# Projecting q, k and z of the first layer by four heads: tokens on partitions, 512 weight columns moving, the results turned by VectorE and transfers

## The chip, the cores and the metric

The kernel runs on one core of one Trainium2 chip, in one launch. The metric is the device time of that launch in microseconds (us); a kernel's number is the median of its runs. Engines are named as the profile names them: PE is TensorE (PEld its weight loads), DVE is VectorE, ACT is ScalarE, POOL is GpSimd, SP is SyncE, which here issues the weight loads.

## What is computed

One step of a two-layer trunk in float32, for 384 tokens (256 prompt tokens of one new stream, and 16 new tokens of each of 8 running streams), width 2048. Cut to what matters here:

```python
# layer 0
h  = rmsnorm(x, norm0_g)
p  = h @ w_in0                       # 2048 x 8200: fox q, k, v, z; stick-breaking q, k, v, z; forget logits
fq, fk, fv, fz, logf, sq, sk, sv, sz = split(p)    # 8 heads of 128 on either side
o_fox = softmax(fq fk^T * scale + F_q - F_k) @ fv  # F: running sum of logf; causal; cached keys and values
o_sb  = stick_breaking(sq, sk) @ sv                # exp(log_sigmoid(z) + reverse running sum of log_sigmoid(-z))
mix = concat(o_fox * silu(fz), o_sb * silu(sz))
x   = x + mix @ w_out0
# layer 1
u, v, z = split(rmsnorm(x, norm1_g) @ w_in1)       # 3 x 4096
x = x + (u * (w_sp @ layernorm(v) + b_sp) * silu(z)) @ w_out1
y = rmsnorm(x, final_g)
```

The outputs are y, the new keys, values and log forget gates, and the normalised v rows of the running streams.

## The kernel before

Every dense product runs as three matmuls on halves of the operands: both operands are split into a rounded part `hi` and a remainder `lo`, and hi·hi, hi·lo and lo·hi are added up in one bank of the accumulator memory. ACT makes `hi` (L80, L86), DVE makes `lo` (L82, L87). Weights come in pieces of 256 KB by SP's queue (`wload`, L73; five buffers) and are split into `whi` and `wlo` (four buffers each). The normalised input is kept transposed, as sixteen blocks of 128 features by 384 tokens (`hhi`, `hlo`).

Layer 0 is worked through in eight pairs of heads (`pair(g)`, L348): g 0 to 3 are fox, 4 to 7 stick-breaking. For q, k and z a pair calls `dense_T` (L89): a 128 by 128 block of weights is stationary, the 384 tokens move, and two banks take the two heads; the result stands with the head's features on partitions, as the scores need it. It is evicted by DVE, with the rows' scale `rstd_bc` (the reciprocal root mean square, spread over all partitions by L147 to L153). Keys are also needed with tokens on partitions, for the output: `natural` (L368) transposes 32 by 32 blocks on DVE and writes the result out with 16 transfers. Values come from `values_first` (L327; 256 columns, the first two pairs) or `dense_nat` (L108; 512 columns moving, for two pairs at once), whose result has tokens on partitions.

`head` (L431) makes the scores (L455 to L460), turns them into probabilities (fox: L472 to L483, with the division by the row's sum in L483; stick-breaking: L485 to L496), transposes these on PE (L500), copies them out (`PT`, L502) and multiplies by the cached and new values (L508 to L521). The part for the running streams (`od`) is copied (L515 or L517) and transposed by PE (L518), so that `mx` has the head's features on partitions. At the end of a pair `mx` is multiplied by silu(z) (L425) and split into the blocks `mixhi`, `mixlo` (L426, by L86 and L87). The out-projection (L563) calls `dense_nat` four times over these blocks.

The accumulator memory is two pools of four banks: `d` for dense products, `a` for all else. The blocks `slot` are a pool of 16 buffers of 128 by 1536. Each engine works through its own list in order; the list is fixed when the kernel is built, by a scheduler that runs a model of the program. `tc.issue_after(i)` puts an instruction behind `i` in it.

In layer 1 the gated products are turned as follows (L673 to L684): DVE transposes the 32 by 32 blocks of a 128 by 1536 tile (`trn`, L674), sixteen transfers from POOL's queue, each 32 partitions by 12 by 32, put the blocks in place (`gTt`, L678), and ACT and DVE split the result (L683, L684).

Of the kernel before, what the change touches and what calls it, by code (L numbers as in the profile page):

```python
# [15 lines left out]
P = 128  # L16
# [10 lines left out]
NEG = -1.0e30  # L27

# [3 lines left out]
def f32(ap):  # L32
    return ap.bitcast(F32)
# [3 lines left out]
def tile_hybrid_step(  # L37
# [18 lines left out]
    splits = []  # L56
# [19 lines left out]
    def wunit(src, nk, ncols, raw=None):  # L76
# [3 lines left out]
        S.activation(hi, raw, AF.Copy)  # L80
        lo = wp.tile([P, WPITCH], F32R, tag="wlo", name=nm("wlo"))[:, :512].rearrange("p (k c) -> p k c", k=nk)
        splits.append(V.tensor_tensor(out=lo, in0=raw, in1=f32(hi), op=ALU.subtract).ins)  # L82
        return hi, lo
# [5 lines left out]
    def dense_T(w, c0, hhi, hlo, raws=(), after=None):  # L89
        out = [dbank(), dbank()]  # L90
        for u in range(KT // 2):
            with ExitStack() as order:
                if after:
                    for i in after[2 * u]:
                        order.enter_context(tc.issue_after(i.ins))
                hi, lo = wunit(w[u * 256:(u + 1) * 256, c0:c0 + 256], 2, 256, raws[u] if u < len(raws) else None)
            for kk in range(2):
                k = 2 * u + kk
                h, l = hhi[k // 4][:, k % 4, :], hlo[k // 4][:, k % 4, :]
                for cb in range(2):  # L100
                    o = out[cb][:, :T]
                    cs = slice(cb * P, (cb + 1) * P)
                    PE.matmul(o, lhsT=hi[:, kk, cs], rhs=h, start=(k == 0), stop=False)  # L103
                    PE.matmul(o, lhsT=hi[:, kk, cs], rhs=l, start=False, stop=False)  # L104
                    PE.matmul(o, lhsT=lo[:, kk, cs], rhs=h, start=False, stop=(k == KT - 1))  # L105
        return out

    def dense_nat(w, k0, c0, his, los, nk=None, between=None):  # L108

        nk = nk or len(his)  # L110
        out = [dbank() for _ in range(NT)]
        for kp in range(0, nk, 2):
            if between and kp in between:
                with tc.issue_after(splits[-1]):
                    between[kp]()
            ws = [wunit(w[(k0 + k) * P:(k0 + k + 1) * P, c0:c0 + 512], 1, 512) for k in (kp, kp + 1)]
            for tb in range(NT):
                t = slice(tb * P, (tb + 1) * P)
                for j in range(2):
                    k = kp + j  # L120
                    hi, lo = ws[j]
                    o = out[tb]
                    PE.matmul(o, lhsT=his[k][:, t], rhs=hi[:, 0, :], start=(k == 0), stop=False)  # L123
                    PE.matmul(o, lhsT=his[k][:, t], rhs=lo[:, 0, :], start=False, stop=False)  # L124
                    PE.matmul(o, lhsT=los[k][:, t], rhs=hi[:, 0, :], start=False, stop=(k == nk - 1))  # L125
        return out
# [8 lines left out]
    rstd_bc = cpool.tile([P, T], F32, name="rstd_bc")  # L135
# [3 lines left out]
    cpool.tile([P, 104], F32, name="apad")  # L139
# [7 lines left out]
    def calc_rstd_bc(pool):  # L147
        diag = pool.tile([P, T], F32, tag="z", name=nm("rdiag"))
        for tb in range(NT):
            V.tensor_scalar(out=diag[:, tb * P:(tb + 1) * P], in0=ident, scalar1=rstd[:, tb:tb + 1], scalar2=None, op0=ALU.mult)  # L150
        b = bank()
        PE.matmul(b[:, :T], lhsT=ones, rhs=diag, start=True, stop=True)
        S.activation(rstd_bc, b[:, :T], AF.Copy)  # L153

# [4 lines left out]
    def load_x(dst, c0, n):  # L159
        nc.sync.dma_start(dst[:, :2, :], xp_view[:, :, c0:c0 + n])  # L160
        nc.sync.dma_start(dst[:, 2, :], xview[2][:, c0:c0 + n])

    def transpose_scaled(src, gcol, hi, lo):

        b = bank()
        for tb in range(NT):
            PE.transpose(b[:, tb * P:(tb + 1) * P], src[tb], ident)
        return (S.activation(hi, b[:, :T], AF.Copy, scale=gcol),
                V.scalar_tensor_tensor(out=lo, in0=b[:, :T], scalar=gcol, in1=f32(hi), op0=ALU.mult, op1=ALU.subtract))


    with ExitStack() as l0:
# [4 lines left out]
        nc.sync.dma_start(graw[:, 0, :], norm0_g.rearrange("(k p) -> k p", p=P))  # L177
# [6 lines left out]
        xs, raws = [], []  # L184
        for c in range(4):
            x_t = slot(F32).rearrange("p (t c) -> p t c", t=NT)
            for j in range(2):
                load_x(x_t[:, :, j * 256:(j + 1) * 256], c * 512 + j * 256, 256)
                if len(raws) < 5:
                    u = len(raws)  # L190
                    raws.append(wload(w_in0[u * 256:(u + 1) * 256, 1024:1280], 2, 256))
            xs.append(x_t)
        hhi, hlo, done = [], [], []
        with tc.issue_after(gains(0).ins):
            for c in range(4):
                hi, lo = slot(), slot()
                hi, lo = hi.rearrange("p (k t) -> p k t", k=4), lo.rearrange("p (k t) -> p k t", k=4)
                for kk in range(4):
                    k = 4 * c + kk
                    done.append(transpose_scaled([xs[c][:, tb, kk * P:(kk + 1) * P] for tb in range(NT)], gT[:, k:k + 1], hi[:, kk, :], lo[:, kk, :]))  # L200
                hhi.append(hi)
                hlo.append(lo)
            first = dense_T(w_in0, 1024, hhi, hlo, raws, done)
        with tc.issue_after(done[-1][0].ins), tc.issue_after(done[-1][1].ins):
            for c in range(4):
                for tb in range(NT):
# [3 lines left out]
                    else:  # L210
                        sq = lp.tile([P, NT * 256], F32, tag="knat", bufs=1, name=nm("sq"))[:, :512]
# [15 lines left out]
        sums = lp.tile([P, NT * P], F32, tag="sg", bufs=1, name="sums")  # L227
# [44 lines left out]
        V.tensor_copy(wf[:, 0, 0:1], hlo[1][:, 3, 0:1].bitcast(F32))  # L272
# [49 lines left out]
        vprev = [None]  # L322
# [25 lines left out]
        def pair(g):  # L348
            fox = g < 4
            hp = g % 4  # L350
            base = (0 if fox else 4096) + hp * 256
            kc, vc = (c_fox_k, c_fox_v) if fox else (c_sb_k, c_sb_v)
            ko_p, vo_p, ko_s, vo_s = (fk_p, fv_p, fk_s, fv_s) if fox else (sk_p, sv_p, sk_s, sv_s)
            h0 = 2 * hp

            kcache = lp.tile([P, 2, 8 * P], F32, tag="kcache", bufs=1, name=nm("kcache"))
            vcache = lp.tile([P, 8, 256], F32, tag="vcache", bufs=1, name=nm("vcache"))
            def project(what, c0):
                o = first if c0 == 1024 else dense_T(w_in0, c0, hhi, hlo)
                t = lp.tile([P, 2, T], F32, tag=what, bufs=2 if what == "kT" else 1, name=nm(what))  # L360
                for cb in range(2):
                    if what == "qT":
                        V.scalar_tensor_tensor(out=t[:, cb, :], in0=o[cb][:, :T], scalar=ATTN_SCALE, in1=rstd_bc, op0=ALU.mult, op1=ALU.mult)
                    else:
                        V.tensor_tensor(out=t[:, cb, :], in0=o[cb][:, :T], in1=rstd_bc, op=ALU.mult)
                return t

            def natural(src, o_p, o_s):  # L368

                nat = lp.tile([P, 2, T // 32, 32], F32, tag="knat", bufs=1, name=nm("knat"))  # L370
                V.transpose(out=nat.rearrange("p h a d -> p (h a d)"), in_=src.rearrange("p h t -> p (h t)"))  # L371
                o_p = o_p[0].rearrange("(a p) h d -> p h a d", p=32)
                o_s = o_s.rearrange("b q h d -> (b q) h d").rearrange("(a p) h d -> p h a d", p=32)
                for j in range(4):
                    js = slice(32 * j, 32 * j + 32)
                    for hh in range(2):
                        G.dma_start(o_p[:, h0 + hh, :, js], nat[js, hh, :8, :])  # L377
                        G.dma_start(o_s[:, h0 + hh, :, js], nat[js, hh, 8:, :])  # L378

            kT = project("kT", base + 1024)  # L380
            natural(kT, ko_p, ko_s)
            if g < 2:
                nv, vnat = 256, lp.tile([P, NT, 256], F32, tag="vnat", name=nm("vnat"))
                o = values_first(base + 2048, g == 0)
            elif g % 2 == 0:
                nv, vnat = 512, lp.tile([P, NT, 512], F32, tag="vnat", name=nm("vnat"))
                o = dense_nat(w_in0, 0, base + 2048, [hk(hhi, k) for k in range(KT)], [hk(hlo, k) for k in range(KT)])
            else:
                nv, vnat = 0, vprev[0]
# [137 lines left out]
        for g in range(8):  # L527
            pair(g)
# [263 lines left out]
```

## Time and profile before

| | |
|---|---|
| runs of the kernel | 1830.46 us median of 3 (1829.74 to 1831.8) |
| the profiled execution's own time | 1831.22 us |
| its span, first to last instruction | 1829.5 us |
| granted clock of PE | 0.999 |
| busy: PE, DVE, ACT, POOL | 1811.7, 932.8, 715.3, 345.2 us |
| dense matmuls with 384 columns moving | 2304 (L103, L104, L105, 768 each) |
| dense matmuls with 512 columns moving | 5472 (L123, L124, L125, 1824 each) |
| moved by DMA | 276.25 MB, 151 GB/s over the span |

The profile shows one execution. A row of its groups reads: line, engine, operation, output<-input, shapes, number; then busy time in us and the mean in ns of one; then the idle time of that engine just before, with what ended it. In a timeline a row begins with its start and its length in us. Matmuls overlap, so the length of one is not its cost: the distance from one start to the next is.

### The profile page before, as it was taken

The numbers are of one execution on the slowest core, as the hardware profiler recorded it, in microseconds if no ns is written. First come the engines' busy times: TensorE is split into PE (matmuls) and PEld (weight loads), VectorE is DVE, ScalarE is ACT, GpSimd is POOL, SyncE is SP. The second block draws the span as 40 slices with busy tenths as digits, with TensorE's granted clock in tenths as the row PEclk, the third lists the DMA queues.
The fourth block names the chain that finished last, engine by engine and source line by source line (L and its number), as shares of the span: only waits on it lengthen the run. The fifth ranks groups of instructions, "written<-read, shape, count | busy, mean of one in ns | idle before, by whom it ended". The sixth has DMA issues, their size and how long they took to land. (4 is left out here: it accounts for less than half of the span.)

```text
span 1829.5 us, 25641 instructions
## 1 busy us (share of the span) xinstructions
PE 1811.7 (99%) x9217; PEld 1565.4 (86%) x9217; DVE 932.8 (51%) x1570; ACT 715.3 (39%) x1275; POOL 345.2 (19%) x559
## 2 busy tenths in 40 slices
PE   8999999999999999999999999999999999999997
PEld 7999899899899888888888888888888888888886
DVE  6466365456646644543443544554543563455366
ACT  5354343444535534443333333333323333333334
POOL 2553233213212002200300111320120210220020
PEclk9999999999999999999999999999999999999999
DMA  6776566565555467744544445554444554455453
GB/s 185 190 181 151 171 148 166 144 165 144 157 149 156 142 175 204 199 127 129 139 130 127 133 137 151 146 144 139 148 139 132 150 155 127 144 144 150 144 146 130
DMA packets 181871, 276.25 MB, mean 151 GB/s; under 512 B 22520, under 2 KB 87984, under 8 KB 181744
## 3 DMA queue, kind: packets, MB, share of 16 engines
q1 hardware_dynamic: 152752, 226.42, 43.1%
q0 software_dynamic: 21792, 43.87, 9.5%
q10 hardware_dynamic: 7200, 4.33, 0.7%
q8 instruction: 72, 1.18, 0.3%
q14 instruction: 55, 0.45, 0.1%
HBM read 253.50 MB, written 14.74 MB: 147 GB/s over the span
## 5 line engine op out<-in xcount | busy, mean ns | idle before, releaser
L82 DVE TENSOR_TENSOR wlo<-raw,whi 128x512 fp32r<-128x512 f32 x800 | 551.2, 695 | 767.6 <-ACT whi L80 766.4
L80 ACT ACTIVATE whi<-raw 128x512 fp32r<-128x512 f32 x800 | 504.2, 631 | 921.5 <-PE d L125 727.9
L124 PE MATMUL d<-wlo,slot 128*128 128x512 f32 x1824 | 711.7, 391 | 0.2
L125 PE MATMUL d<-whi,slot 128*128 128x512 f32 x1824 | 706.2, 389 | 0.0
L123 PE MATMUL d<-whi,slot 128*128 128x512 f32 x1824 | 632.3, 390 | 0.9 <-ACT slot L557 0.5
L123 PEld LDWEIGHTS d<-whi,slot 128*128 128x128 f32 x1824 | 342.4, 188 | 73.2 <-ACT slot L557 1.0
L124 PEld LDWEIGHTS d<-wlo,slot 128*128 128x128 f32 x1824 | 342.5, 188 | 71.7 <-DVE wlo L82 1.0
L125 PEld LDWEIGHTS d<-whi,slot 128*128 128x128 f32 x1824 | 342.5, 188 | 70.9
L105 PE MATMUL d<-slot,wlo 128*128 128x384 f32 x768 | 259.4, 338 | 0.0
L104 PE MATMUL d<-slot,whi 128*128 128x384 f32 x768 | 258.7, 337 | 0.0
L103 PE MATMUL d<-slot,whi 128*128 128x384 f32 x768 | 258.3, 337 | 0.0
L678 POOL DMA_DIRECT2D gTt<-trn x128 | 78.1, 618 | 446.4 <-issue 263.8
L105 PEld LDWEIGHTS d<-slot,wlo 128*128 128x128 f32 x768 | 144.2, 188 | 6.1 <-issue 6.0
L104 PEld LDWEIGHTS d<-slot,whi 128*128 128x128 f32 x768 | 144.6, 188 | 0.5 <-issue 0.4
L103 PEld LDWEIGHTS d<-slot,whi 128*128 128x128 f32 x768 | 144.5, 188 | 0.4
L377 POOL DMA_DIRECT2D out_dram<-knat x64 | 38.1, 596 | 113.1 <-DVE knat L371 112.9
L639 POOL DMA_DIRECT2D wr<-in_w_sp_dram x64 | 35.0, 554 | 26.7 <-DVE wT L643 25.6
L633 DVE TENSOR_TENSOR slot<-d,slot 128x512 f32<-128x512 f32 x48 | 32.2, 687 | 12.6 <-PE d L125 12.6
L404 POOL DMA_DIRECT2D kcache<-in_cache_sb_k_dram x32 | 25.0, 790 | 71.4 <-DVE KT L451 57.5
L378 POOL DMA_DIRECT2D out_dram<-knat x64 | 36.1, 563 | 0.0
L545 POOL DMA_DIRECT2D blk<-h1d x12 | 11.0, 922 | 129.0 <-DMA h1d<-slot 99.6
L596 POOL DMA_DIRECT2D slot<-in_sgu_ln_g_dram x8 | 4.5, 568 | 135.4 <-PE d L125 135.4
(220 smaller groups left out, 1189.6 us busy)
## 6 DMA issues: line engine op xcount, KB each, us to landing
raw<-in_w_in_dram SPq DMA_DIRECT2D x640, 256.0 KB, 2.8
raw<-in_w_out_dram SPq DMA_DIRECT2D x192, 256.0 KB, 3.3
gTt<-trn POOLq DMA_DIRECT2D x128, 48.0 KB, 3.4
kcache<-in_cache_fox_k_dram POOLq DMA_DIRECT2D x32, 128.0 KB, 5.3
vcache<-in_cache_fox_v_dram POOLq DMA_DIRECT2D x4, 1024.0 KB, 8.0
kcache<-in_cache_sb_k_dram POOLq DMA_DIRECT2D x32, 128.0 KB, 4.7
vcache<-in_cache_sb_v_dram POOLq DMA_DIRECT2D x4, 1024.0 KB, 6.6
h1d<-slot ACTq DMA_DIRECT2D x12, 256.0 KB, 2.8
```

Source lines behind the costliest of these rows:

```text
L80: S.activation(hi, raw, AF.Copy)
L82: splits.append(V.tensor_tensor(out=lo, in0=raw, in1=f32(hi), op=ALU.subtract).ins)
L103: PE.matmul(o, lhsT=hi[:, kk, cs], rhs=h, start=(k == 0), stop=False)
L104: PE.matmul(o, lhsT=hi[:, kk, cs], rhs=l, start=False, stop=False)
L105: PE.matmul(o, lhsT=lo[:, kk, cs], rhs=h, start=False, stop=(k == KT - 1))
L123: PE.matmul(o, lhsT=his[k][:, t], rhs=hi[:, 0, :], start=(k == 0), stop=False)
L124: PE.matmul(o, lhsT=his[k][:, t], rhs=lo[:, 0, :], start=False, stop=False)
L125: PE.matmul(o, lhsT=los[k][:, t], rhs=hi[:, 0, :], start=False, stop=(k == nk - 1))
L377: G.dma_start(o_p[:, h0 + hh, :, js], nat[js, hh, :8, :])
L378: G.dma_start(o_s[:, h0 + hh, :, js], nat[js, hh, 8:, :])
L639: G.dma_start(wr[js, 0, :].rearrange("p (a s) -> p a s", s=32), w_sp[g, :, js].rearrange("(a p) s -> p a s", p=32))
L678: G.dma_start(gT[32 * j:32 * j + 32, :, 32 * a:32 * a + 32], trn[32 * a:32 * a + 32, :, 32 * j:32 * j + 32])
```

## The change

It has five parts.

1. `dense_T` goes, and q, k and z are projected by `dense_nat`, four heads at a time (`quad(g)`, g 0 to 3): a block of 128 tokens is stationary, 512 weight columns move, and three banks hold the three blocks of tokens. ACT evicts them with the row scale (`evict`, L400 of the new kernel) into a `slot`. `turn` then does what layer 1 does: one DVE transpose of 128 by 1536 (L124) and sixteen POOL transfers (L127), for keys, queries and, at the end of a quad, for the mixed output (`mT`), which is then split by ACT (L473) and DVE (L474). `rstd_bc` goes. Keys go out with two transfers (L403, L404).
2. In `head` the output is made with tokens on partitions (three matmuls, L559 to L561; DVE writes it into `mixn`, L564 or L567, where the fox rows are divided by their sums). L483, L518 and the two ACT copies L523 and L524 go.
3. The opening is put in order by hand (`then`): transposes of x, splits and products by pairs of k, the first products beginning after two of the sixteen blocks; `graw` and two pieces of x are loaded from ACT's queue.
4. The first two of the four out-projections are taken in two steps (`early`: the twelve blocks of quads 0 to 2, with the second in banks of pool `a`; `rest`: the last four).
5. At the end three of the last weight pieces are loaded early by POOL, and the last splits lie between or behind the products of `out1(24, 4)`.

The core of the diff:

```diff
-    def dense_T(w, c0, hhi, hlo, raws=(), after=None):
...
-                    PE.matmul(o, lhsT=hi[:, kk, cs], rhs=h, start=(k == 0), stop=False)
-                    PE.matmul(o, lhsT=hi[:, kk, cs], rhs=l, start=False, stop=False)
-                    PE.matmul(o, lhsT=lo[:, kk, cs], rhs=h, start=False, stop=(k == KT - 1))
+    def products(out, his, los, ws, kp, tbs, first, last):
...
+                PE.matmul(o, lhsT=his[k][:, t], rhs=hi[:, 0, :], start=(k == first), stop=False)
+                PE.matmul(o, lhsT=his[k][:, t], rhs=lo[:, 0, :], start=False, stop=False)
+                mm = PE.matmul(o, lhsT=los[k][:, t], rhs=hi[:, 0, :], start=False, stop=(k == last))
...
+    def turn(src, dst, trn=None):
+        trn = slot(F32).rearrange("p (x d) -> p x d", d=P) if trn is None else trn
+        V.transpose(out=trn.rearrange("p x d -> p (x d)"), in_=src.rearrange("p t d -> p (t d)"))
+        for j in range(4):
+            for a in range(4):
+                G.dma_start(dst[32 * j:32 * j + 32, :, 32 * a:32 * a + 32], trn[32 * a:32 * a + 32, :, 32 * j:32 * j + 32])
...
-        calc_rstd_bc(lp)
+        V.tensor_scalar(out=rstdq, in0=rstd, scalar1=ATTN_SCALE, scalar2=None, op0=ALU.mult)
...
+            def project(c0):
+                return first if c0 == 1024 else dense_nat(w_in0, 0, c0, h0h, h0l)
+            def evict(o, dst, scale, n=512):
+                for tb in range(NT):
+                    S.activation(dst[:, tb, :], o[tb][:, :n], AF.Copy, scale=scale[:, tb:tb + 1])
...
+            def turned(c0, scale, tag, outs=None):
+                nat = slot(F32).rearrange("p (t c) -> p t c", t=NT)
+                evict(project(c0), nat, scale)
+                if outs:
+                    store(nat, *outs)
+                t = lp.tile([P, NT * 4, P], F32, tag=tag, bufs=1, name=nm(tag))
+                turn(nat, t)
+                return t.rearrange("p (t h) q -> p h t q", h=4), nat
...
+            for hh in range(4):
+                hs = slice(hh * P, hh * P + P)
+                head(g, h0 + hh, kT[:, hh], vnat[:, :, hs], qT[:, hh], *cached(hh), mixn[:, :, hs])
+            zn = big("gz")
+            evict(project(base + 3072), zn, rstd)
...
+                V.tensor_tensor(out=z, in0=z, in1=mixn[:, tb, :], op=ALU.mult)
+            t = lp.tile([P, NT * 4, P], F32, tag="qT", bufs=1, name=nm("mT"))
+            turn(zn, t)
...
+            for k in range(4):
+                h3 = mixhi[g][:, k, :].rearrange("p (t q) -> p t q", q=P)
+                S.activation(h3, mT[:, k], AF.Copy)
...
-            PE.transpose(od[:, P:2 * P], os_, ident)
...
-        for g in range(8):
-            pair(g)
+        for g in range(4):
+            quad(g)
...
+        early, rest = range(0, 12, 2), range(12, KT, 2)
+        outs = [[dbank() for _ in range(NT)], [bank() for _ in range(NT)]]
```

How it moves instructions, at three places. First PE at the end of a group of heads. Before, behind the second head of pair 0 (L520 and L521 are the products of its prompt part), the dense products of pair 1's values go on in banks that are already theirs:

```order
L508 MATMUL a_1055<-vnat_494,PT_1053 32x128 x4
L512 MATMUL a_1055<-vcache_472,PT_1053 32x128 x8
L520 MATMUL a_1071<-PT_1040,vnat_494 128x256
L521 MATMUL a_1071<-PT_1040,vnat_494 128x128
L344 MATMUL d_1411<-wlo_1585,slot_206 128x256
L345 MATMUL d_1411<-whi_1584,slot_207 128x256
```

Now, at the end of quad 0, its fourth head (scores L503 to L508, transposes L545, products L553 to L561) and what follows it; `d_2211` to `d_2213` are the banks of the query projection of quad 1, and `d_1943` to `d_1945` (not in these rows) those of its key projection, complete by then:

```order
L508 MATMUL a_1589<-KT_1584,qT_1308 32x256 x2
L101 MATMUL d_2211<-whi_2246,slot_120 128x512
L102 MATMUL d_2211<-wlo_2248,slot_120 128x512
L103 MATMUL d_2211<-whi_2246,slot_121 128x512
L101 MATMUL d_2211<-whi_2252,slot_120 128x512
L102 MATMUL d_2211<-wlo_2254,slot_120 128x512
L103 MATMUL d_2211<-whi_2252,slot_121 128x512
L545 MATMUL a_1605<-ident,pr_1601 128x128 x3
L545 MATMUL a_1618<-ident,pr_1615 128x128 x3
```

```order
L559 MATMUL a_1637<-vnat_590,PT_1609 128x128
L560 MATMUL a_1637<-vnat_590,PT_1609 128x128
L561 MATMUL a_1637<-vnat_590,PT_1609 128x128
L101 MATMUL d_2212<-whi_2216,slot_120 128x512
L102 MATMUL d_2212<-wlo_2218,slot_120 128x512
```

Six dense matmuls stand between the fourth head's scores and its transposes, and behind its last product comes the first one into `d_2212`, a bank that the key projection held: pool `d` has four.

Second, ACT at the same place: the copies of the fourth head, the split of the turned output, the three evictions of the key projection, a weight split.

```order
L547 ACTIVATE PT_1609<-a_1605 128x384
L547 ACTIVATE PT_1622<-a_1618 128x384
L473 ACTIVATE slot_1932<-mT_1913 128x384 x4
L400 ACTIVATE slot_1942<-d_1943,rstd 128x512
L400 ACTIVATE slot_1942<-d_1944,rstd 128x512
L400 ACTIVATE slot_1942<-d_1945,rstd 128x512
L84 ACTIVATE whi_2276<-raw_2274 128x512
```

The evictions stand behind the split of `mT`, which needs all sixteen transfers. Before, at the end of pair 0, the evictions (here of pair 1's values) stood ahead of the split of the last head's output (`slot_1233<-mx_1074`):

```order
L523 ACTIVATE mx_1074<-a_1071 128x256
L392 ACTIVATE vnat_1410<-d_1411,rstd 128x256
L392 ACTIVATE vnat_1410<-d_1412,rstd 128x256
L392 ACTIVATE vnat_1410<-d_1413,rstd 128x256
L80 ACTIVATE whi_1678<-raw_1676 128x512
L524 ACTIVATE mx_1074<-a_1055 128x128
L86 ACTIVATE slot_1233<-mx_1074 128x384
```

Third, PE's opening, before (L167 are transposes of x, `d_232` and `d_233` the first two banks):

```order
L167 MATMUL a_142<-ident,slot_95 128x128
L167 MATMUL a_148<-ident,slot_95 128x128
L167 MATMUL a_156<-ident,slot_104 128x128 x3
L167 MATMUL a_162<-ident,slot_104 128x128 x3
L167 MATMUL a_168<-ident,slot_104 128x128 x3
L103 MATMUL d_232<-slot_128,whi_234 128x384
```

and now (L211 are the transposes):

```order
L211 MATMUL a_131<-ident,slot_95 128x128 x3
L211 MATMUL a_137<-ident,slot_95 128x128 x3
L101 MATMUL d_128<-whi_143,slot_120 128x512
L102 MATMUL d_128<-wlo_145,slot_120 128x512
L103 MATMUL d_128<-whi_143,slot_121 128x512
L101 MATMUL d_128<-whi_147,slot_120 128x512
```

The first dense product stands behind two blocks' transposes, where it stood behind seven.

More of the change, by code (lines that the diff above doesn't have):

```diff
@@ L27 @@
 NEG = -1.0e30
+APAD = 96
 WPITCH = 576
@@ new lines, in dense_nat @@
+    def dense_nat(w, k0, c0, his, los, nk=None, between=None, out=None, ks=None):
+        nk = nk or len(his)
+        out = out or [dbank() for _ in range(NT)]
+        for kp in range(0, nk, 2) if ks is None else ks:
+            behind = ()
+            if between and kp in between:
+                with tc.issue_after(splits[-1]), tc.issue_after(highs[-1]):
+                    behind = between[kp]() or ()
+            ws = [wunit(w[(k0 + k) * P:(k0 + k + 1) * P, c0:c0 + 512], 1, 512, behind=behind) for k in (kp, kp + 1)]
+            products(out, his, los, ws, kp, range(NT), 0, nk - 1)
+        return out
@@ L145, in calc_rstd, with load_x @@
         G.tensor_tensor(out=rstd, in0=tot, in1=ex, op=ALU.pow)
[L147 to L153, printed above, removed]
     xview = [x_prompt[0, 0:P, :], x_prompt[0, P:2 * P, :], x_sample.rearrange("b q c -> (b q) c")]
     xp_view = x_prompt.rearrange("o (t p) c -> p (o t) c", p=P)
-    def load_x(dst, c0, n):
+    def load_x(dst, c0, n, q=None):
         nc.sync.dma_start(dst[:, :2, :], xp_view[:, :, c0:c0 + n])
[L161 to L169, printed above, removed]
+        (q or nc.sync).dma_start(dst[:, 2, :], xview[2][:, c0:c0 + n])
     with ExitStack() as l0:
@@ L194, in tile_hybrid_step @@
[L194 to L203, printed above, removed]
+        tail = {}
@@ new lines, in tile_hybrid_step, with x_transposes @@
+        load_piece(0)
+        load_raw()
+        load_raw()
+        load_piece(1)
+        load_raw()
+        load_raw()
+        load_piece(2)
+        load_raw()
+        load_piece(3)
+        tail["DVE"] = gains(0).ins
+        hhi, hlo = [], []
+        for c in range(4):
+            hhi.append(slot().rearrange("p (k t) -> p k t", k=4))
+            hlo.append(slot().rearrange("p (k t) -> p k t", k=4))
+        def x_transposes(k):
+            b = bank()
+            for tb in range(NT):
+                then("PE", lambda: PE.transpose(b[:, tb * P:(tb + 1) * P], xs[k // 4][:, tb, k % 4 * P:k % 4 * P + P], ident))
+            gcol = gT[:, k:k + 1]
+            hi, lo = hhi[k // 4][:, k % 4, :], hlo[k // 4][:, k % 4, :]
+            return (then("ACT", lambda: S.activation(hi, b[:, :T], AF.Copy, scale=gcol)),
+                    then("DVE", lambda: V.scalar_tensor_tensor(out=lo, in0=b[:, :T], scalar=gcol, in1=f32(hi), op0=ALU.mult, op1=ALU.subtract)))
@@ new lines, in first_unit @@
+        def first_unit(k):
+            hi = wp.tile([P, WPITCH], F32R, tag="whi", name=nm("whi"))[:, :512].rearrange("p (k c) -> p k c", k=1)
+            then("ACT", lambda: S.activation(hi, raws[k], AF.Copy))
+            lo = wp.tile([P, WPITCH], F32R, tag="wlo", name=nm("wlo"))[:, :512].rearrange("p (k c) -> p k c", k=1)
+            splits.append(then("DVE", lambda: V.tensor_tensor(out=lo, in0=raws[k], in1=f32(hi), op=ALU.subtract)).ins)
+            return hi, lo
+        h0h = [hhi[k // 4][:, k % 4, :] for k in range(KT)]
```

329 lines of the change are left out of this document (163 added, 166 removed).

## The prediction

> **What bounds the kernel now.** I read the page's first two parts, then the waits of PE, then timelines of PE at places where the change acts.
>
> ```profile
> span 1829.5 us, 25641 instructions
> PE 1811.7 (99%) x9217; PEld 1565.4 (86%) x9217; DVE 932.8 (51%) x1570; ACT 715.3 (39%) x1275; POOL 345.2 (19%) x559
> PE   8999999999999999999999999999999999999997
> PE a L167 <- DMA slot<-in_x_prompt_dram: 4.8, 3, 2.6
> PE a L181 <- DMA graw<-in_norm_g_dram: 2.5, 1, 2.5
> PE d L721 <- DVE slot L633: 1.3, 1, 1.3
> PE d L123 <- ACT slot L557: 0.5, 1, 0.5
> PE d L123 <- DVE slot L567: 0.3, 1, 0.3
> ```
>
> PE is full from the opening to the tail. Its waits add up to 9.4 us (4.8 + 2.5 + 1.3 + 0.5 + 0.3), and the last three are all there is behind the opening. So the change can win only by fewer or cheaper matmuls, an earlier start or a shorter tail, and it loses whatever new idle time it gives PE. The page's span stands 1.7 us below the execution's own 1831.22 us, and that 0.8 us above the median of the runs; I sum against 1831.2 and take 0.8 off at the end. A difference of 0.2% (3.7 us) is about what a measurement of this kernel can tell from none.
>
> **Dense matmuls.** The price is the pitch from start to start.
>
> ```profile
> 71.10 0.33 PE L105 MATMUL d<-slot,wlo 128*128 128x384 f32 x1
> ...
> 72.83 0.33 PE L103 MATMUL d<-slot,whi 128*128 128x384 f32 x1
> 899.89 0.39 PE L124 MATMUL d<-wlo,slot 128*128 128x512 f32 x1
> ...
> 903.29 0.39 PE L123 MATMUL d<-whi,slot 128*128 128x512 f32 x1
> L105 PE MATMUL d<-slot,wlo 128*128 128x384 f32 x768 | 259.4, 338 | 0.0
> L518 PE MATMUL a<-ident,os 128*128 128x128 f32 x16 | 4.3, 271 | 0.0
> ```
>
> Between the first two rows lie ten steps, 0.173 us each; between the next two fifteen, 0.2267 us each. Removed: 3 x 768 = 2304 steps of 0.1733, 399.3 us. Added: 12 projections of 16 x 9 = 144 products, 1728 of 0.2267, 391.7 us. That is **−7.5**: per column moved the two differ little (0.451 and 0.443 ns). The sixteen L518 go; alone they show 4.3 us, overlapped perhaps 0.11 each: **−1.8** (0 to −4.3). L520 with its two products and L559 to L561 move the same 384 columns: nothing. L483 and L523/L524 leave engines that are half idle: nothing.
>
> **The opening.**
>
> ```profile
> 0.79 1.28 ACT L47 ACT_TABLE_LOAD   x1 [0.79 <-PEq L779]
> 0.80 0.39 SPq L177 DMA_DIRECT2D graw<-in_norm_g_dram  x1
> 4.41 1.54 PE L167 MATMUL a<-ident,slot 128*128 128x128 f32 x6 [1.67 <-DMA slot<-in_x_prompt_dram]
> ...
> 12.73 0.67 PE L103 MATMUL d<-slot,whi 128*128 128x384 f32 x1
> 13.20 0.52 PE L104 MATMUL d<-slot,whi 128*128 128x384 f32 x1
> 13.52 0.52 PE L103 MATMUL d<-slot,whi 128*128 128x384 f32 x1
> 13.84 0.44 PE L104 MATMUL d<-slot,whi 128*128 128x384 f32 x1
> L153 ACT ACTIVATE rstd_bc<-a 128x384 f32<-128x384 f32 x1 | 0.5, 493 | 4.8 <-PE a L152 4.8
> ```
>
> The first six transposes start at 4.41, dense work at 12.73. Now products may follow those six and one round of splits. `graw`, issued at 0.80 by SP, is now issued by ACT behind its table load, which ends at 2.07, and the first piece of the running streams' x behind it: up to 1.3 later. Together about 8.5, **−4** (0, if loads hold it, to −5). In exchange the first eviction needs `rstd`, which comes after the squares, and only one bank is free meanwhile; before, ACT had 4.8 us of waiting for the same scale. **+2.5** (0 to 4.8). The tail's 1.3 and the two small gaps may go: **−2** (0 to −2.1).
>
> **The end of a quad.** This decides. By the new order ACT reaches the evictions of the next quad's keys (L400) only behind the split of `mT` (L473), and PE's next product needs a bank that such an eviction frees. So PE waits through the whole turn of the fourth head's output, and behind ACT's wait stand also the weight splits. The turn is in the trace, in layer 1:
>
> ```profile
> 1087.21 1.77 DVE L674 STREAM_TRANSPOSE trn<-gate 128x1536 f32<-128x1536 f32 x1
> 1089.28 9.75 POOL L678 DMA_DIRECT2D gTt<-trn x16 [53.37 <-DVE trn L674]
> L678 POOL DMA_DIRECT2D gTt<-trn x128 | 78.1, 618 | 446.4 <-issue 263.8 <-DVE wlo L82 129.2 <-DVE trn L674 53.4
> DMA to landing us min/median/max: 1.9/3.4/5.0
> 1783.75 1.75 ACT L683 ACTIVATE slot<-gTt 128x384 fp32r<-128x384 f32 x4
> L586 ACT ACTIVATE vt<-d,rstd 128x512 f32<-128x512 f32 x24 | 16.3, 690 | 12.0 <-PE d L125 12.0
> L633 DVE TENSOR_TENSOR slot<-d,slot 128x512 f32<-128x512 f32 x48 | 32.2, 687 | 12.6 <-PE d L125 12.6
> L515 DVE TENSOR_SCALAR os<-a,st 128x128 f32<-128x128 f32 x8 | 2.8, 349 | 4.1 <-PE a L512 4.1
> ```
>
> From the fourth head's last product: three writes of 0.349 and three products with silu(z) of 0.687 on DVE, of which about 0.4 lies beside PE's last matmuls, 2.7; the transpose 1.77; sixteen transfers 9.75; the last one's landing 3.4 less its own issue, 2.8; the split of four blocks 1.75; one eviction 0.69. That is 19.5, with five handovers between engines **20 us** (17.5 with the shortest landing and no handovers, 22 with the longest). Layer 1 pays nothing for it, since PE has other products there.
>
> What PE still has to do meanwhile, from the new order: at the end of quad 0 nothing, its twelve products into the one free bank being used up; of quad 1, 57 products, 12.9 us; of quad 2 nothing again. Hence 20, 7.1 and 20.
>
> The fourth head itself loses its cover too, since its scores and transposes stand almost side by side:
>
> ```profile
> 115.06 0.60 PE L455 MATMUL a<-kT,qT 128*128 128x256 f32 x2
> ...
> 116.03 0.64 PE L460 MATMUL a<-KT,qT 128*32 128x256 f32 x8
> ...
> 120.07 0.60 ACT L476 ACTIVATE pr<-z,st 128x384 f32<-128x384 f32 x1
> ...
> 124.72 0.87 ACT L502 ACTIVATE PT<-a 128x384 f32<-128x384 f32 x2 [1.12 <-PE a L500]
> 413.70 0.60 PE L455 MATMUL a<-kT,qT 128*128 128x256 f32 x2
> ...
> 420.88 0.53 ACT L496 ACTIVATE pr<-z 128x384 f32<-128x384 f32 x1 [1.05 <-DVE z L494]
> ...
> 426.09 0.51 ACT L496 ACTIVATE pr<-z 128x384 f32<-128x384 f32 x1
> ```
>
> A fox head takes 5.6 us from its first score to its last exponential (115.06 to 120.67); less 1.6 of scores (to 116.67) and six products of 0.2267 that is 2.6, and 0.5 for the copy of the probabilities: 3 at quad 0. A stick-breaking head took 7.7 to the first exponential and 12.9 to the second. The bare case, quad 3's last head, has no dense product between scores and transposes: I take 10.5, between the two, less 1.6 for scores, plus 0.5: 9.5 (7 to 12). In quad 2 some 35 products lie beside it, 8 us: 2.4. Quad 3's own turn lies beside the early products of the second out-projection, 12 blocks by 9, 108 of 0.2267 or 24.5 us behind the last head: I take that as covered, at up to 4 if not.
>
> Together 3 + 20 + 7.1 + 2.4 + 20 + 9.5 = **+62**.
>
> Behind such a wait PE is slow at first. In the opening's rows the 384-column products from 13.20 to 13.84 stand 0.32 apart instead of 0.173, though the granted clock reads 1.00 there; the three steps from 12.73 cost 1.11 instead of 0.52. I take 1 us for each of four long waits, **+4** (2.4 to 7). The Trainium skill's page "TensorE: Matmul & The Clock Gate", section "Why this matters for your kernels", says to leave no PE-idle gaps over about 3 us between bursts, else PE goes back to half its rate; it speaks against this change. The opening's pitch agrees. If, by that page's Part 1, half the rate lasts for 3.4 us each time, 1.7 us are lost each time, and the sum would be 2.8 us higher.
>
> **Sum.** −7.5 − 1.8 − 4 + 2.5 − 2 + 62 + 4 = +53.2: 1831.2 + 53.2 = 1884.4, less 0.8: **1883.6 us**. The low ends (three turns 2.5 shorter, the bare heads 2.5 shorter, clock 2.4, no `rstd` wait, L518 at 4.3) give about 1867; the high ends (turns 2 longer, heads 2.5 longer, clock 7, no gain in opening and tail, `rstd` 4.8, quad 3's turn 4) about 1907.
>
> **Rivals.**
>
> Hidden turns, faster: were the four turns and last heads beside other products, as layer 1's are, only −7.5 − 1.8 − 4 + 2.5 − 2 = −12.8 would be left, 1817.6. It needs 20 us of products, some 88 of them, between a fourth head's last product and the first one into a bank still held. For it: L678's transfers in layer 1 cost PE no wait. Against: the order has 0, 57 and 0. 0.05.
>
> Cheap issue: if the sixteen transfers were issued beside each other, so that the turn took 1.77 and one landing of 3.4, each of the three waits would be some 9 shorter (the second gone): 62 − 9 − 7.1 − 9 = 37, about 1858.5. The row of L678 speaks against it, 618 ns each on POOL one after the other, 9.75 for sixteen. The Trainium skill's page "DMA: Bandwidth & Descriptors", section "Issuing engines are not separate DMA queues", says that the time to initiate is usually small relative to the DMA itself; for these small transfers the trace disagrees, 9.75 us of issue against 3.4 of landing. 0.06.
>
> POOL held up, slower still: ahead of `mT`'s transfers POOL's list holds the next quad's cache loads.
>
> ```profile
> L404 POOL DMA_DIRECT2D kcache<-in_cache_fox_k_dram x32 | 25.1, 794 | 13.0 <-DVE KT L451 12.3 <-DVE vcache L401 0.7
> L406 POOL DMA_DIRECT2D vcache<-in_cache_fox_v_dram x4 | 3.7, 923 | 15.6 <-PE a L512 15.6
> ```
>
> Four of 0.794 and one of 0.923 make a head's set, 4.1 us. Its value load waits for the fourth head's last cached product; if the set is issued only then, up to 4.1 at each of three quads come in front, less the 4.5 of DVE work beside it: nothing if one set, but with two sets 3.7 each, 11 in all, 1894.7. With the ends of the other terms, over 1908. 0.06.
>
> No difference: gains and waits cancel if the waits are 13 us in all, which no row suggests: 0.02.
>
> **How the numbers follow.** Forecast 0.81, cheap issue 0.06, POOL 0.06, hidden 0.05, cancelled 0.02. The forecast's bounds, 1867 to 1907, with half of each neighbouring case make the range 1856 to 1908. Faster by over 0.2%: 0.05. Within: 0.02. Slower: 0.93.
>
> **What would show it.** In the profile after, PE's waits name ACT's L400 for about 20, 7 and 20 us at the ends of quads 0, 1 and 2, with ACT idle until the transfers of `mT` and POOL busy with L127 for 9.75 us before; DVE or ACT of the last stick-breaking head holds L545 for about 9 us. Dense products start near 8.5 us. PE's busy share falls to about 96%. The forecast is wrong if those waits are under 10 us, if new waits of that size stand elsewhere, or if products of 512 columns in layer 0 don't come at 0.227 us.

## The result, and the profile after

The changed kernel takes 1888.93 us (median of 4 runs, 1888.49 to 1889.66) against 1830.49 before (4 runs): a ratio of 1.0318, 95% interval [1.0305, 1.0331]. It is 58 us slower; 1883.6 was forecast.

The page of the profile after, its span, busy times, the slices of PE and of its granted clock, and the longest waits of PE (us in all, times, longest):

```profile
span 1887.9 us, 24617 instructions
PE 1816.4 (96%) x8655; PEld 1497.2 (79%) x8655; DVE 922.8 (49%) x1541; ACT 726.2 (38%) x1294; POOL 401.2 (21%) x640
PE   8999599989959989999999999999999999999998
PEclk9999799999979989999999999999999999999999
PE d L101 <- ACT slot L400: 41.8, 3, 18.0
PE a L545 <- ACT pr L541: 10.0, 3, 4.3
...
PE a L553 <- ACT PT L547: 1.7, 3, 0.6
PE a L545 <- ACT pr L524: 1.4, 2, 1.0
```

PE's first 17 slices are layer 0. Four of them have dips now, two deep (5) and two shallow (8), and the granted clock dips in three of the four. Three waits for the evictions of L400 make 41.8 us, and the waits for a last head's L541, L547 and L524 another 13.1.

The timeline of all engines at the end of quad 0 shows the chain as the list of ACT implied it (start, length, engine, line):

```profile
210.35 0.63 PE L561 MATMUL a<-vnat,PT 128*128 128x128 f32 x2
213.36 1.78 DVE L124 STREAM_TRANSPOSE slot<-gz 128x1536 f32<-128x1536 f32 x1
215.44 9.76 POOL L127 DMA_DIRECT2D mT<-slot  x16 [0.93 <-DVE slot L124]
226.61 1.76 ACT L473 ACTIVATE slot<-mT 128x384 fp32r<-128x384 f32 x4 [18.13 <-DMA mT<-slot]
228.28 1.82 ACT L400 ACTIVATE slot<-d,rstd 128x512 f32<-128x512 f32 x3
229.00 0.80 PE L101 MATMUL d<-whi,slot 128*128 128x512 f32 x1 [18.02 <-ACT slot L400]
```

ACT stands for 18.13 us before the split of `mT`, with finished evictions behind it in its list; PE's first product comes 0.72 after the first of these begins. At the end of quad 1, where 57 products lay beside, the wait is 6.15.

The windows of that place and of the end of quad 1 (length, busy and number on PE, PEld, DVE, ACT, POOL, then the granted clock), and PE's timeline behind the wait:

```profile
210.50:229.00 18.50, 0.48 (x4) 0.19 (x2) 5.96 (x10) 2.39 (x6) 13.74 (x21) 0.50 0.38 95
229.00:233.00 4.00, 4.00 (x9) 3.14 (x10) 1.91 (x2) 1.10 (x2) 2.11 (x4) 0.50 0.46 186
384.30:390.00 5.70, 5.70 (x13) 4.45 (x14) 1.90 (x2) 1.10 (x2) 3.81 (x7) 0.50 0.42 156
229.59 0.63 PE L102 MATMUL d<-wlo,slot 128*128 128x512 f32 x1
230.02 0.63 PE L103 MATMUL d<-whi,slot 128*128 128x512 f32 x1
...
233.78 0.39 PE L101 MATMUL d<-whi,slot 128*128 128x512 f32 x1
...
235.82 0.39 PE L101 MATMUL d<-whi,slot 128*128 128x512 f32 x1
```

For 4 us behind quad 0's wait the granted clock is 0.50 and products come 0.43 apart; then nine steps take 2.04 us, 0.227 each, the pitch of layer 1 before the change. Behind the waits of quads 1 and 2 it lasts 5.7 us, behind quad 3's last head 2.8.

The last head of quad 3 stands bare, as forecast:

```profile
695.83 0.90 PE L545 MATMUL a<-ident,pr 128*128 128x128 f32 x3 [4.30 <-ACT pr L541]
700.45 0.90 PE L545 MATMUL a<-ident,pr 128*128 128x128 f32 x3 [3.73 <-ACT pr L541]
```

### The profile page after: what moved, and what is told of

Its sections match the earlier page's. It is cut to its first block, busy times and chain, and to the rows that moved or that the text cites. A ratio compares the mean times of both kernels' runs of the same rounds, so it can differ in the third digit from the quotient of the medians.

```text
span 1887.9 us, 24617 instructions
## 1 busy us (share of the span) xinstructions
PE 1816.4 (96%) x8655; PEld 1497.2 (79%) x8655; DVE 922.8 (49%) x1541; ACT 726.2 (38%) x1294; POOL 401.2 (21%) x640
## 5 line engine op out<-in xcount | busy, mean ns | idle before, releaser
L102 PE MATMUL d<-wlo,slot 128*128 128x512 f32 x2352 | 923.7, 394 | 0.1
L103 PE MATMUL d<-whi,slot 128*128 128x512 f32 x2352 | 916.7, 391 | 0.0
L101 PE MATMUL d<-whi,slot 128*128 128x512 f32 x2352 | 826.1, 393 | 43.0 <-ACT slot L400 41.8
L101 PEld LDWEIGHTS d<-whi,slot 128*128 128x128 f32 x2352 | 443.8, 189 | 138.9 <-ACT slot L400 42.7
L102 PEld LDWEIGHTS d<-wlo,slot 128*128 128x128 f32 x2352 | 444.2, 189 | 94.0 <-issue 1.2
L103 PEld LDWEIGHTS d<-whi,slot 128*128 128x128 f32 x2352 | 443.9, 189 | 94.1 <-issue 2.5
L127 POOL DMA_DIRECT2D gTt<-trn x128 | 78.2, 618 | 446.4 <-issue 262.8
L127 POOL DMA_DIRECT2D qT<-slot x64 | 39.1, 619 | 83.1 <-DVE slot L124 81.7
L127 POOL DMA_DIRECT2D mT<-slot x64 | 39.1, 618 | 49.8 <-issue 40.3
L127 POOL DMA_DIRECT2D kT<-slot x64 | 39.3, 621 | 8.1 <-DVE slot L124 3.2
L545 PE MATMUL a<-ident,pr 128*128 128x128 f32 x96 | 17.8, 284 | 11.5 <-ACT pr L541 10.0
L380 PE MATMUL d<-wlo,slot 128*128 128x264 f32 (+1 forms) x96 | 27.2, 286 | 0.6 <-DVE wlo L91 0.6
L379 PE MATMUL d<-whi,slot 128*128 128x264 f32 (+1 forms) x96 | 26.7, 287 | 0.5 <-ACT slot L400 0.5
L381 PE MATMUL d<-whi,slot 128*128 128x264 f32 (+1 forms) x96 | 26.8, 283 | 0.0
L545 PEld LDWEIGHTS a<-ident,pr 128*128 128x128 f32 x96 | 12.7, 144 | 17.2 <-ACT pr L541 11.3
```

Of the source, the lines that this page charges most:

```text
L103: mm = PE.matmul(o, lhsT=los[k][:, t], rhs=hi[:, 0, :], start=False, stop=(k == last))
L127: G.dma_start(dst[32 * j:32 * j + 32, :, 32 * a:32 * a + 32], trn[32 * a:32 * a + 32, :, 32 * j:32 * j + 32])
L379: PE.matmul(o, lhsT=h, rhs=hi[:, kk, :n], start=(k == 0), stop=False)
L380: PE.matmul(o, lhsT=h, rhs=lo[:, kk, :n], start=False, stop=False)
L381: PE.matmul(o, lhsT=l, rhs=hi[:, kk, :n], start=False, stop=(k == KT - 1))
L545: PE.transpose(b[:, o:o + P], pr[:, j * P:(j + 1) * P], ident)
```

## The experiments

Each is an edit of the changed kernel, run beside the kernel before on the same chip. The chips differed between the groups of experiments, and the kernel before took 1830.5 to 1831.45 us on them, so a difference between two groups is good to about 1 us. Theory A is the prediction's: ACT's list has a quad's next evictions behind the split of its turned output.

**The split behind the key evictions.** Nothing but the place of one block:

```diff
             kT, nat = turned(base + 1024, rstd, "kT", (ko_p, ko_s))
+            if pending:
+                pending.pop()()
...
-            mixhi.append(slot().rearrange("p (k t) -> p k t", k=4))
...
+            def finish():
+                mixhi.append(slot().rearrange("p (k t) -> p k t", k=4))
...
+            pending.append(finish)
+            if g == 3:
+                pending.pop()()
```

> The new kernel with the split of a quad's turned output (mT) written behind the next quad's key evictions, so that ACT's list has the evictions first; nothing else moves. Theory A (the order of ACT's list): PE's three waits for L400, 41.8 us together, go, and with them the slow stretch behind each, some 1.9 us: 1888.9 - 41.8 - 5.7 = about 1841 us. The waits inside the last heads of quads 0, 2 and 3 (13 us) stay. Rival B (buffers): the evictions' destination is a buffer that the turn still holds, so that their place in the list does not matter: about 1889, with the same waits.

1842.43 us (1.0061 of before, [1.0045, 1.0078]). PE's waits for the evictions are gone from the list, at the end of quad 0 a dense product follows the last one of the head at once, and those inside the last heads stay:

```profile
PE a L553 <- ACT pr L549: 10.0, 3, 4.3
...
210.42 0.63 PE L569 MATMUL a<-vnat,PT 128*128 128x128 f32 x2
210.71 0.77 PE L101 MATMUL d<-whi,slot 128*128 128x512 f32 x1
```

So the order alone cost 46.5 of the 58 us, the slow products behind the waits included. The buffers (rival B) did not hold the evictions.

**Half of the issue on ACT.** In `turn`, for `mT` only:

```diff
-                G.dma_start(dst[32 * j:32 * j + 32, :, 32 * a:32 * a + 32], ...
+                (other if other and a % 2 else G).dma_start(dst[32 * j:32 * j + 32, :, 32 * a:32 * a + 32], ...
...
-            turn(zn, t)
+            turn(zn, t, other=nc.scalar)
```

> The new kernel with 8 of the 16 transfers of each quad's mT issued by ACT instead of POOL. If the issue one after the other on POOL lies on the waits' path (theory A's working: 9.76 us for 16), each of the three waits is shorter by up to 4.9 us less what ACT's issue costs: 1875 to 1882 us, POOL's row of 16 falls to 8 in 4.9 us. Rival (cheap issue: the transfers' landing sets the end, not their issue): no change, 1889.

1876.24 us (two runs), 12.7 less. The waits fell from 41.8 to 30.2: by 2.5, 5.4 and 3.8 us at the ends of quads 0, 1 and 2. At the end of quad 0 the sixteen issues take 5.5 us instead of 9.8, and the split begins 2.4 behind the last one instead of 1.4:

```profile
PE d L101 <- ACT slot L400: 30.2, 3, 15.5
213.85 4.87 POOL L127 DMA_DIRECT2D mT<-slot  x8 [1.81 <-DVE slot L124]
213.59 5.48 ACTq L127 DMA_DIRECT2D mT<-slot  x8
```

Issue one after the other was on the path; the rival of cheap issue falls.

**Idle work on PE during the waits.**

```diff
+            if g < 3:
+                idle = bank()
+                with tc.issue_after(last_o[0].ins):
+                    for _ in range((150, 50, 150)[g]):
+                        PE.transpose(idle[:, :P], ident, ident)
```

> The new kernel with idle work on PE during the three waits: 150, 50 and 150 transposes of the identity behind the last product of the fourth head of quads 0, 1 and 2, into a bank that nobody reads. The waits' length stays. Theory (clock): the 512-column products behind a wait came 0.43 us apart for 4 us because PE had been idle; with PE kept busy they come 0.227 apart at once and the granted clock stays at 1.0: 5 to 6 us less, about 1883. Rival (the pitch of 0.43 has another cause, such as splits that come late): no gain, 1889.

1883.50 us (two runs), 5.4 less, though PE's first product at the end of quad 0 comes no earlier from the head's last one (228.36 - 209.70 = 18.7 us; in the changed kernel 229.00 - 210.35 = 18.7):

```profile
209.70 0.64 PE L567 MATMUL a<-vnat,PT 128*128 128x128 f32 x2
210.13 17.11 PE L458 MATMUL a<-ident 128*128 128x128 f32 x150
228.36 0.50 PE L101 MATMUL d<-whi,slot 128*128 128x512 f32 x1 [1.11 <-ACT slot L401]
229.00:233.00 4.00, 4.00 (x19) 3.30 (x18) 2.02 (x2) 1.32 (x3) 2.76 (x5) 1.00 0.54 209
```

19 products start in those 4 us instead of 9, at a clock of 1.00. So the slow stretch came of PE's idling and not of late splits. By the medians it costs 1.8 us a wait; in the trace of the changed kernel the three stretches cost 2.0, 2.8 and 2.8. Their length differs between executions: 9, 13 and 13 slow products there, 6, 12 and 12 in the next experiment's trace.

**The out-projection as before.** `early` and `rest` replaced by four plain calls.

> The new kernel with its fourth part undone: the four out-projections one after the other as before, none in two steps. If the early products cover the turn of quad 3 (as the prediction took it), PE now waits for L473 there as at the ends of quads 0 and 2: some 18 to 20 us and a slow stretch more, about 1909 us. If something else covers it, about 1889.

1905.11 us (one run). A fourth long wait appears behind quad 3's last head:

```profile
PE d L101 <- ACT slot L473: 15.9, 1, 15.9
719.94 0.79 PE L101 MATMUL d<-whi,slot 128*128 128x512 f32 x1 [15.90 <-ACT slot L473]
```

The early products do cover quad 3's turn, as the prediction took it, and are worth 16 us, by this single run.

**Key projection ahead of the fourth head.** On top of the first experiment:

```diff
+                if hh == 3 and g < 3:
+                    ahead.append(natural((512, 4096, 4608)[g] + 1024, rstd))
                 head(g, h0 + hh, kT[:, hh], vnat[:, :, hs], qT[:, hh], *cached(hh), mixn[:, :, hs])
```

> On top of the split behind the evictions (1842.4 us): the next quad's key projection and its evictions are written ahead of the fourth head, so that the query projection's products can run beside that head. By theory A the waits left in the fourth heads of quads 0 and 2 (some 2.6 and 3.0 us, with PE slow behind them) go, and that of quad 3 (9.6 us and a slow stretch) stays: 1834 to 1838 us. If these waits have another cause than missing dense work: about 1842.

A miss: 1854.71 us (1.0129 of before, [1.0116, 1.0142]), 12 more than without. The last heads of quads 0 and 2 were covered, but what covered them was missing later. Two heads of quad 3 now stood bare (waits for L556 of 15.6 in all, against 10.0 for L549), and the old wait came back one projection on, at the query evictions (`rstdq`):

```profile
PE a L560 <- ACT pr L556: 15.6, 4, 4.3
PE d L101 <- ACT slot L402: 6.6, 3, 6.1
537.53 1.76 ACT L484 ACTIVATE slot<-mT 128x384 fp32r<-128x384 f32 x4 [5.55 <-DMA kT<-slot]
539.20 1.82 ACT L402 ACTIVATE slot<-d,rstdq 128x512 f32<-128x512 f32 x3
```

**A fox head last.** On top of that `for g in (0, 2, 3, 1)`, with the out-projection's early blocks chosen to match.

> On top of that the quads run in the order 0, 2, 3, 1, so that the last head, which has least dense work beside it, is a fox head, whose chain took 5.6 us against 7.7 to 12.9 of a stick-breaking head. The wait of 9.6 us at the last head falls to 1 to 3 and its slow stretch goes: 9 us less than the kernel with keys early, 1825 to 1829 us, at or below the kernel before (1830.5). If a bare last head costs the same whichever it is: no gain, 1836.

1844.94 us (1.0076 of before, [1.0064, 1.0088]): 9.8 less than with the keys early, as expected of the step, but above the range, whose start had been taken from the expectation before. The bare heads' waits fell to about 1; what is left is the wait at the query evictions, `PE d L101 <- ACT slot L402`, now 15.7 us in three.

**The opening, twice.** On top of that, singly: 36 transposes of the identity ahead of the first dense product (16, 10 and 10, between the real ones); and `graw` and the first two pieces of x back on SP's queue.

> On top of that 36 transposes of the identity that nobody reads, on PE in the idle time of the opening, ahead of the first dense product. Theory (clock): the first dozen dense products came 0.43 apart because PE had been idle; kept busy, they come 0.227 apart from the start, 2 us less than without. Rival (the opening is bound by the loads of x and weights, so that faster products only wait later): less than 0.5 us.

> The fox-last kernel with the gains and the first two pieces of the running streams' x loaded from SP's queue as before, instead of ACT's behind its table load. The first transpose then starts near 2.5 instead of 3.9 us. If that load sets the start of dense work, up to 1.3 us less; if the other pieces and weights do (SP's queue gets three more issues of about 0.45 us each ahead), the same or up to 1 us more.

1842.59 us (six runs, 1840.79 to 1848.57) and 1841.99 us (four runs, 1841.62 to 1842.41): 2.4 and 3.0 less than 1844.94, the first not clear of its own spread. With the idle work the first products are fast from the start (see 9.88 and 10.12), with SP's loads they start 1.6 earlier than without (6.85 after 8.42) and are slow (8.60 and 9.03):

```profile
9.88 0.40 PE L101 MATMUL d<-whi,slot 128*128 128x512 f32 x1
10.12 0.39 PE L102 MATMUL d<-wlo,slot 128*128 128x512 f32 x1
...
8.60 0.63 PE L101 MATMUL d<-whi,slot 128*128 128x512 f32 x1
9.03 0.63 PE L102 MATMUL d<-wlo,slot 128*128 128x512 f32 x1
```

Not all of the 2.4 and 3.0 was won in the opening. The first matmul of the forget products, behind the first projection, stands as follows without either edit, with the idle work and with SP's loads:

```profile
48.02 0.28 PE L381 MATMUL d<-whi,slot 128*128 128x264 f32 x1
...
47.03 0.28 PE L391 MATMUL d<-whi,slot 128*128 128x264 f32 x1
...
46.68 0.28 PE L381 MATMUL d<-whi,slot 128*128 128x264 f32 x1
```

At this point 1.0 us and 1.3 were won, by one trace of each; both stand ahead of all seven traces with the opening as it was (47.56 to 49.60). That is less than the 2 us expected of the idle work and as much as was expected of the loads. Much of the rest lies in the slow stretches behind the two query evictions, which neither edit touches: 14 and 12 slow products without either, 7 and 10 with the idle work, 7 and 7 with SP's loads.

**The split behind the query evictions.** With SP's loads (the edit below is against that kernel); then with the idle work of the opening as well.

```diff
-            if pending:
-                pending.pop()()
...
-            qT, _ = turned(base, rstdq, "qT")
+            qnat = natural(base, rstdq)
+            if pending:
+                pending.pop()()
+            qT, _ = turned(base, rstdq, "qT", None, qnat)
```

> The fox-last kernel with SP's loads in the opening (1842.0 us), and the split of a quad's turned output one step later: behind the next quad's query evictions instead of its key evictions. Theory A (order): the waits that the keys-early kernels showed for L402 (16.4 us in all, two of 8) are the same wait as before, moved on to the query evictions, which stood behind the split; they go with their slow stretches: 1842 - 16.4 - 3.8 = about 1822 us, below the kernel before. If the query evictions wait for something else, such as the buffers: about 1842.

> The same with the 36 transposes that nobody reads in the opening. Warm opening and SP's loads gave 2.4 and 3.0 us singly. If they act on different things (PE's clock; the time at which the first pieces land), they add up: 2 to 2.5 us less than the kernel without, about 1820. If both only fill the same gap: less than 1 us.

1832.75 us (1.0011 of before, [1.0002, 1.0020]): the evictions' waits are gone, but only 9.2 of the expected 20 us came. In the last quad the heads begin at 596.0 us instead of 591.4, and the last two find no dense product beside them: waits of 4.8 for L540 and 1.2 for L563, and a slow stretch. The queries' turn begins late there:

```profile
568.67 1.77 DVE L124 STREAM_TRANSPOSE slot<-slot 128x1536 f32<-128x1536 f32 x1
```

The buffer that it shares with `mT` was free at 554.3, when DVE's part of the split ended, and POOL had issued the keys' transfers by 557.2. The transpose stands behind weight splits in DVE's list; why the list has it so late is not shown. Both together in the opening: 1833.64, no gain where 2 to 2.5 us was expected. There the idle work itself delays the first product, which starts at 9.14 instead of 7.08.

**Half of the issue on ACT, for queries and mixed output.** On top of the split behind the query evictions, with SP's loads:

> The kernel with the split behind the query evictions (1832.8 us), with 8 of the 16 transfers of each turn of queries and of the mixed output issued by ACT. In that kernel the last quad's heads begin late, since the queries' turn waits for the split of the quad before (they share a buffer) and for POOL, and its last two heads have no dense product beside them: waits of 6.5 us and a slow stretch, some 13 in all. If issue on POOL sets when the heads begin, the two turns are some 4 us shorter each, dense products are left for the last heads, and most of the 13 us go: 1821 to 1826 us. If ACT's issue instead holds up the weight splits, or the landing sets the end: 1831 or more.

1825.88 us, 0.9972 of before, [0.9960, 0.9984], as expected: a version that beats both kernels. Its page and its longest waits:

```profile
PE 1805.2 (99%) x8655; PEld 1486.9 (81%) x8655; DVE 922.1 (51%) x1541; ACT 721.5 (40%) x1294; POOL 362.7 (20%) x576
PE d L101 <- ACT whi L84: 3.2, 4, 1.1
```

No wait of layer 0 behind the opening is over 1.1 us. The last two heads have dense products beside them again. With the later split, the earlier keys, the order of the quads, SP's loads and the shared issue together, the change gains 5.6 us, where its dense products promised 7.5. Of the 63 us between the changed kernel and this one the first experiment's split gave 46.5; what each of the other edits is worth alone was not measured.

## Why the prediction was right

Point by point, the term of the sum, then what was measured; gaps and pitches are taken from start to start in the trace.

- *Turns, 20 + 7.1 + 20.* 18.3, 6.3 and 17.8 between starts, by the mechanism named; writing the split later took them away. They are shorter mainly since the split began 1.4 us behind the end of the last issue (226.61 after 225.20), where 2.8 was taken from layer 1's median landing.
- *Last heads, 3 + 2.4 + 9.5.* 2.6, 2.9 and 9.6.
- *Dense, −7.5.* Without waits and slow stretches, layer 0's dense products take 637.5 us before (2304 of 384 columns and 1008 of 512) and 629.5 after (2736 of 512): −8.0.
- *L518, −1.8; the output products, nothing.* A dense product with an L518 behind it and the next one took 0.12 us more than two products alone (187.40 to 187.87 before, against twice 0.1733), sixteen times 1.9: as forecast. Six output products take 0.77 where four took 0.76, but 1.65 and 1.30 in the last heads of quads 0 and 3, at the slow clock.
- *Slow PE behind a wait, +4.* The term that was mis-sized: 8.9, above even its high end of 7. Behind the four waits 9, 13, 13 and 6 dense products come slowly, which costs 2.0, 2.8, 2.8 and 1.4 us. The low value had been read in the opening before, where 21 transposes ran ahead of the first product; that they had used up most of the slow time is likely, but not tested. By the Trainium skill's page "TensorE: Matmul & The Clock Gate" (Part 1, half the rate for about 3.4 us) the estimate was 1.7 a wait; the trace agrees with the half rate, a granted clock of 0.50, but it lasts 4.0, 5.7, 5.7 and 2.8 us.
- *Early out-projection covers quad 3.* It does; 16 us more without it.
- *Opening, −4 and +2.5.* The first product came at 8.65 as forecast, but little was won. The first matmul of the forget products, a point that both kernels pass:

```profile
33.13 0.40 PE L343 MATMUL d<-whi,slot 128*128 128x264 f32 x2
49.60 0.28 PE L379 MATMUL d<-whi,slot 128*128 128x264 f32 x1
```

  Less the first projection at its pitch (96 of 0.1733, 144 of 0.2267) these are 16.5 and 17.0: half a microsecond lost. Executions differ here: in the seven traces that have this opening the point lies between 47.56 and 49.60, with 6 to 10 slow products ahead of it, which is between 1.6 won and 0.5 lost. The step that failed is "dense work starts 4 us earlier, so 4 us are won": of the 48 transposes 21 lay ahead of the first product and now 6, so that fifteen more (0.11 each) follow it, and the first ten products were slow, 2.6 us in all against 0.6 before. The wait for `rstd` was 0.5, not 2.5, which makes up for less than half of that error: −1.5 was forecast for both, and 1.0 measured.
- *Tail, −2.* The wait for L633 and the two small gaps are gone from PE's list.
- *The rivals.* Hidden turns: the list had no products there, and the waits came. Cheap issue: refuted by the half on ACT. The page "DMA: Bandwidth & Descriptors" of the Trainium skill (section "Issuing engines are not separate DMA queues") says that a second issuing engine saves only issue time, and the trace agrees: 4.3 us of issue, and no earlier landing behind it. That issue is small beside the transfer holds here for a single one, 0.62 us against 3.4 to landing in layer 1; the prediction's "disagrees" set sixteen issues in a row against one landing. POOL held up: at the end of quad 0 the next quad's value load was issued at 213.59 and ended at 214.51, before the transpose did at 215.14, so nothing came in front.

The books close where layer 1 begins:

```profile
751.49 0.39 PE L123 MATMUL d<-whi,slot 128*128 128x512 f32 x1
812.24 0.39 PE L101 MATMUL d<-whi,slot 128*128 128x512 f32 x1
```

60.7 us later. Of these 42.4 are turns, 15.1 last heads, 8.9 slow products behind waits, 1.0 the opening with its `rstd` wait, −1.9 the L518 and −8.0 the cheaper products, 57.5 together. The other 3.2 belong to no term of the sum; the slow output products of the last heads are part of them. Behind this point 2.3 are won back, the tail's term.

That the forecast came within 5 us is in part luck. Its turns were 4.7 too dear and its slow products 4.9 too cheap, which cancels; the opening's 2.5 and the 3.2 without a term make up the rest. The mechanism and the size of the largest term, the turns that PE waits out, were right.

## What to carry to other kernels

The turn cost PE no wait in layer 1, and some 18 us where finished evictions stood behind its consumer in ACT's list: before moving data through a turn of 18 us, look at what its consumer's engine has next, and at who waits for that. Cover is a fixed stock: giving a waiting head the next projection's products took them from a later head, and a wait mended in one place came back one eviction on. An earlier first matmul is no gain by itself; compare a later common point, less the work at its pitch, and more than one trace of it.

## What the runs showed of the hardware

Short waits slow PE too. In the last head of quad 0 with the split written later, no wait was over 1.04 us, yet the granted clock was 0.50 from 210 to 212 us, and the first dense products behind it (210.71 to 212.13) took 1.42 us for three steps, where 0.68 is usual (the third row is a window, with the granted clock third from its end):

```profile
206.60 0.33 PE L553 MATMUL a<-ident,pr 128*128 128x128 f32 x1 [1.04 <-ACT pr L532]
207.33 0.55 PE L553 MATMUL a<-ident,pr 128*128 128x128 f32 x3 [0.40 <-ACT pr L532]
...
210.00:212.00 2.00, 2.00 (x8) 1.81 (x8) 1.51 (x4) 0.14 (x1) 1.99 (x4) 0.50 0.80 211
...
212.13 0.55 PE L101 MATMUL d<-whi,slot 128*128 128x512 f32 x1
...
212.98 0.39 PE L101 MATMUL d<-whi,slot 128*128 128x512 f32 x1
```

And the granted clock of the profile cannot be trusted in the opening: from 8.65 to 13.00 it reads 1.00 while products come 0.43 apart.

```profile
8.65:13.00 4.35, 4.35 (x13) 3.34 (x14) 1.28 (x3) 0.90 (x2) 0.00 (x0) 1.00 1.03 358
```

Transposes that nobody reads kept PE fast as well as products do: behind 150 of them the clock was 1.00, and 19 products started in 4 us.
